# New weights for the budget that spreads the PEER routing over the expert tiles, and six gathered slots moved behind the routing

## The chip, the cores and the metric

One core of a Trainium2 chip runs one decoder layer as one program. The metric is the device time in microseconds (us) of an execution, the median of three runs of the kernel before. The engines are named as the profile names them: PE is TensorE (PEld its weight loads), DVE is VectorE, ACT is ScalarE, POOL is GpSimd, SP is SyncE, whose queue starts most of the transfers between HBM and SBUF.

## The reference

A layer on 512 tokens of width 1024, in float32: attention beside a Conformer convolution, then the part that this case is about, PEER, then a gated embedding and a last RMSNorm. PEER retrieves from 128 x 128 experts of one neuron each:

```python
q = (xb @ w_q).reshape(P, PEER_HEADS, 2, PEER_DK_HALF)
s = jnp.einsum('phcd,hcnd->phcn', q, sub_keys)
v1, i1 = lax.top_k(s[:, :, 0], 16);  v2, i2 = lax.top_k(s[:, :, 1], 16)
cand = v1[..., :, None] + v2[..., None, :]          # 16 x 16 sums a head
best, pos = lax.top_k(cand.reshape(P, 8, 256), 16)
e, g = cand_idx[pos], softmax(best)                 # 8 x 16 = 128 slots a token
act = gelu(einsum('pd,phkd->phk', xb, u_tab[e]))
out = einsum('phk,phkd->pd', g * act, v_tab[e])
```

## The kernel before, in words

The 512 tokens are four token tiles of 128. Everything up to the scores of the keys is done by some 334 us of the span. From there the kernel does PEER in two ways.

**Token tiles 1 to 3 go dense.** The 16384 experts are 128 expert tiles of 128. For every expert tile, `dense_act` (lines 788 to 799) multiplies its slice of `u_t` by the 384 tokens (24 matmuls into `aps`, three for each product, since each float32 operand is split into a high and a low part) and ACT puts the GELU of it into a tile `act`. Later `dense_out` (line 1054) multiplies the gated `act` by the expert tile's slice of `v_tab` (18 matmuls into `vps`). In front of each, `stage` (line 775) loads the slice (`tr`), ACT rounds it to the high part (`th`) and DVE makes the low part (`tl`, line 144). `act` is a ring of 19 buffers (RING). I write A0, A1, ... for `dense_act` of the k-th expert tile and V0, V1, ... for `dense_out` in its order.

**The gates of the dense way are the routing.** `route` (line 984) is a generator of small pieces for one token tile after the other: `best_keys` (16 pieces: the 16 best of 128 keys, L723 to L728), `topk` (8 pieces for the 8 heads, L859 to L864; then one-hot compares that turn positions into expert numbers, L900 to L911, into a tile `sel` with one buffer). For token tiles 1 to 3 follow three PE transposes (L929 to L931), which ACT copies to `ids` and `gsc` (L933, L936), and 16 halves of a scatter: DVE makes one-hot tiles `o12` (L950) and gated ones `og` (L957), two buffers each, PE multiplies them (`gp`, L977 and L978, 16 matmuls a half), ACT copies the result to `stg` (L979), and SP writes `gd` to HBM (L982).

**Token tile 0 is gathered.** Its 128 slots are fetched row by row by POOL (L808 from `u_tab`, then L819 from `v_tab`), with four buffers `g`; DVE does one pass a row (`gj`, L812, then `acc`, L822): 256 slots in all.

**What sets the order.** The first stage is the loop of lines 998 to 1013: 65 expert tiles A0 to A64, and behind each as much of the routing as a budget allows. `vec` adds up the DVE time of what was written, `mat` the PE time, both from constants and from the weights that the pieces yield; pieces are taken while `vec < pace * mat`, where `pace` is the ratio of the sums expected for the whole stage (line 995). G_EARLY gathered slots are spread over it from the tile G_FROM on. `tiles_later(2)` holds the transposes and the first scatter of a token tile back until two more expert tiles are written; while it does, keys of the next token tile are taken. The transposes and each half's matmuls are tied behind the last matmul of the expert tile written last (`tc.issue_after`, lines 928 and 974). Everything else is an order of priority only: the framework's planner lets an instruction that is ready go ahead of an earlier one that is not, on each engine, at times that it works out itself. `prep_act(e + 2)` stands two tiles ahead of its use.

Written behind the loop, `units` (line 1076 on) are A65, A66, A67, V0, A68, V1, ...: `prep_out` (line 1042) of V0 needs the gates of all three token tiles, loaded from `gd` (`gch`, L1034, three pieces at first), times `act` (`cf`, L1047), split into `ch` (ACT) and `cl` (DVE). The ring has room for A65 and A66 beside the 17 kept tiles; A67 gets its buffer when V0's `cf` has read its own. `background` (line 1068, called after each unit) spreads the remaining gathered slots evenly by weight, G_EARLY of them taken as done.

Of the kernel before, what the change touches and what calls it, by code (L numbers as in the profile page):

```python
# [55 lines left out]
OCH = 8  # L56
PAIR = 2
GBUF = 4
G_EARLY = 6
G_FROM = 20  # L60
EARLY_TOP = (0, 1)
TOP_PACE = 4
ROUTE_V = 237.0
ROUTE_M = 46.0
U_V = 1.2
G_V = 1.25
A_M = 3.9
CONV_PE = (1,)
TAPS = (6, 2, 5, 2)
FILL = (2, 2, 1.5, 1.5, 1, 1, 1, 1)  # L70
# [27 lines left out]
def hymba_layer(ctx, tc, x, xT, p_t, pos, pvec, conv_ln_g, conv_ln_b, w_in, w_uq, w_ukv, w_out,  # L98
# [48 lines left out]
    def split(hi, lo, src, g=None):  # L147
        split_hi(hi, src, g)
        split_lo(lo, src, hi, g)
# [9 lines left out]
    def rows(w, k, c0, c1):  # L159
        return w[k * P:(k + 2) * P, c0:c1].rearrange("(i p) n -> p i n", p=P)  # L160

    def wpair(srcs, n, gains, beside=None):

        r = wst.tile([P, 2, 512], F32, name="wr2", tag="wr")
        hi = wst.tile([P, 2, 512], F32R, name="wh2", tag="wh", bufs=WBUF)
        lo = wst.tile([P, 2, 512], F32R, name="wl2", tag="wl", bufs=WBUF)
        for i in (slice(0, 1), slice(1, 2)) if beside else (slice(0, 2),):
            if beside:
                nc.sync.dma_start(*beside[i.start])
            o = 0  # L170
            for src in srcs:
                w = src.shape[-1]
                nc.sync.dma_start(r[:, i, o:o + w], src[:, i])
                o += w
        if gains is None:
            split(hi[:, :, :n], lo[:, :, :n], r[:, :, :n])
        else:
            for i in range(2):
                split(hi[:, i, :n], lo[:, i, :n], r[:, i, :n], gains[i])
        return hi, lo  # L180
# [6 lines left out]
    with ExitStack() as fs:  # L187
# [414 lines left out]
        for s in range(n_it + 7):  # L602
            if s < n_it:
                t, h = items[s]
# [104 lines left out]
    def new_top(t):  # L709
        tops[t] = (hpool.tile([P, NH, 2, TOPK], F32, name=f"tv{t}", tag="tv", bufs=2),  # L710
                   hpool.tile([P, NH, 2, TOPK], U32, name=f"ti{t}", tag="ti", bufs=2))

    with ExitStack() as fs:
        ps_mm = fs.enter_context(tc.tile_pool(name="ps_mm", bufs=4, space=PSUM))
        mid = fs.enter_context(tc.tile_pool(name="mid", bufs=1))

        def best_keys(t, rs):
            if t not in tops:
                new_top(t)
            s, (tv, ti) = sc[t], tops[t]  # L720
            for r in rs:
                h, c = divmod(r, 2)
                nc.vector.max(out=tv[:, h, c, 0:8], in_=s[:, r])  # L723
                nc.vector.max_index(out=ti[:, h, c, 0:8], in_max=tv[:, h, c, 0:8], in_values=s[:, r])
                nc.vector.match_replace(out=s[:, r], in_to_replace=tv[:, h, c, 0:8], in_values=s[:, r],
                                        imm_value=-3e38)
                nc.vector.max(out=tv[:, h, c, 8:16], in_=s[:, r])
                nc.vector.max_index(out=ti[:, h, c, 8:16], in_max=tv[:, h, c, 8:16], in_values=s[:, r])  # L728
                yield 1.0, 0.0

        early = (i for t in EARLY_TOP for i in best_keys(t, range(8)))


        for g in range(2):
            kraw = mid.tile([P, 4, 2 * NK], F32, name="kraw", tag="kraw")
            nc.vector.memset(kraw, 0.0)
            nc.sync.dma_start(kraw[0:64, :, 0:NK], keys_t[0][:, g * 4:g * 4 + 4])
            nc.sync.dma_start(kraw[64:128, :, NK:], keys_t[1][:, g * 4:g * 4 + 4])
            kbh = mid.tile([P, 4, 2 * NK], F32R, name="kbh", tag="kbh")
            kbl = mid.tile([P, 4, 2 * NK], F32R, name="kbl", tag="kbl")  # L740
            split(kbh, kbl, kraw)
            qTh = mid.tile([P, 4, T], F32R, name="pqh", tag="pqh")
            qTl = mid.tile([P, 4, T], F32R, name="pql", tag="pql")
            ps = [ps_mm.tile([P, 512], F32, name="qps", tag="mm") for _ in range(4)]
            for k2 in range(0, KD, 2):
                if g:
                    for _ in range(TOP_PACE):
                        next(early, None)
                hi, lo = wpair([rows(peer_wq, k2, g * 512, g * 512 + 512)], 512, None)
                for i in range(2):  # L750
                    k = k2 + i
                    for j in range(4):
                        mm3(ps[j], hi[:, i, j * P:(j + 1) * P], lo[:, i, j * P:(j + 1) * P], xnh[:, k], xnl[:, k],
                            k == 0, k == KD - 1)
            for j in range(4):
                split(qTh[:, j], qTl[:, j], ps[j])
            for t in range(NT):
                for j in range(0, 4, 2):
                    h = g * 4 + j
                    ps = ps_mm.tile([P, 512], F32, name="sps", tag="mm")  # L760
                    for i in range(2):
                        mm3(ps[:, i * 256:(i + 1) * 256], qTh[:, j + i, t * P:(t + 1) * P],
                            qTl[:, j + i, t * P:(t + 1) * P], kbh[:, j + i], kbl[:, j + i], True, True)
                    nc.scalar.activation(sc[t][:, 2 * h:2 * h + 4].rearrange("p a n -> p (a n)"), ps, AF.Copy)
        for _ in early:
            pass
# [58 lines left out]
    with ExitStack() as fs:  # L825
# [14 lines left out]
        def tiles_later(n):  # L840

            e = last_tile[0] + n
            while last_tile[0] < e:
                yield None

        def topk(t):
# [11 lines left out]
            for h in range(NH):  # L858
                nc.vector.max(out=bv[:, h, 0:8], in_=cand[:, h])  # L859
                nc.vector.max_index(out=bp[:, h, 0:8], in_max=bv[:, h, 0:8], in_values=cand[:, h])  # L860
                nc.vector.match_replace(out=cand[:, h], in_to_replace=bv[:, h, 0:8], in_values=cand[:, h],
                                        imm_value=-3e38)
                nc.vector.max(out=bv[:, h, 8:16], in_=cand[:, h])
                nc.vector.max_index(out=bp[:, h, 8:16], in_max=bv[:, h, 8:16], in_values=cand[:, h])  # L864
                yield (1.9 if h == 0 else 0.8), 0.0

            ge = tmp.tile([P, NH, TOPK], F32, name="ge", tag="ge")
            nc.vector.tensor_tensor(ge, bv, bv[:, :, 0:1].to_broadcast([P, NH, TOPK]), op=ALU.subtract)
# [26 lines left out]
            for j0, w in ((0, 8), (8, 16)):  # L895
# [14 lines left out]
                for c in range(2):  # L910
# [7 lines left out]
            pg = pg0 if t == 0 else tmp.tile([P, NSL], F32, name="pg", tag="pg")  # L918
            nc.vector.tensor_tensor(pg.rearrange("p (h k) -> p h k", h=NH), ge,
                                    gs.unsqueeze(2).to_broadcast([P, NH, TOPK]), op=ALU.mult)  # L920
            yield 1.0, 0.0
            if t == 0:
                nc.vector.scalar_tensor_tensor(pidx, sel[:, 0], float(NK), sel[:, 1], op0=ALU.mult, op1=ALU.add)
                return
# [17 lines left out]
            for c in range(P // TCH):  # L942
                stg = s8p.tile([P, NK, TCH], F32, name="stg", tag="s8")
                for c0 in range(0, TCH, OCH):
                    cs = slice(c * TCH + c0, c * TCH + c0 + OCH)
                    ng = OCH // PAIR
                    gs0 = cs.start // PAIR
                    o12 = ohp.tile([P, ng, 2, NK, PAIR], F16, name="o12", tag="o12")
                    og = ohp.tile([P, ng, 2, NK, PAIR], F16, name="og", tag="og")
                    nc.vector.tensor_tensor(  # L950
                        o12.rearrange("p g c n q -> p (g c) n q"),
                        iok.unsqueeze(1).to_broadcast([P, 2 * ng, NK, PAIR]),
                        ids[:, gs0:gs0 + ng].rearrange("p g c q -> p (g c) q").unsqueeze(2)
                        .to_broadcast([P, 2 * ng, NK, PAIR]), op=ALU.is_equal)
                    yield 1.1, 0.0

                    nc.vector.tensor_tensor(  # L957
                        og, o12[:, :, 1].unsqueeze(2).to_broadcast([P, ng, 2, NK, PAIR]),
                        ghl[:, gs0:gs0 + ng].unsqueeze(3).to_broadcast([P, ng, 2, NK, PAIR]), op=ALU.mult)
                    late.append((c, c0, stg, o12, og))  # L960
                    if len(late) > LATE:
                        if not started:

                            yield from tiles_later(2)
                            started = True
                        scatter(t, *late.pop(0))
                    yield 1.1, 0.94
            while late:
                scatter(t, *late.pop(0))

# [23 lines left out]
        ngat, vec, mat = 0, 0.0, 0.0  # L994
        pace = (ROUTE_V + U_V * EARLY + G_V * G_EARLY) / (A_M * (EARLY - 2) + ROUTE_M)
        for e in range(AHEAD):
            prep_act(e)
        for e in range(EARLY):
            prep_act(e + AHEAD)
            dense_act(e)  # L1000
            vec += U_V
            mat += A_M
            want = (e + 1 - G_FROM) * G_EARLY / (EARLY - G_FROM)
            while ngat < want:
# [14 lines left out]
    with ExitStack() as fs:  # L1019
# [48 lines left out]
        def background(w):  # L1068
            nonlocal ngat, spent
            spent += w  # L1070
            want = G_EARLY + spent / total * (2 * NSL - G_EARLY)
            while ngat < 2 * NSL and ngat < want:
# [226 lines left out]
```

## Time and profile before

| | |
|---|---|
| median of three runs | 1523.48 us (1522.2 to 1530.78) |
| the profiled execution | 1526.01 us, span 1524.1 us, mean granted clock 0.989 |
| PE busy | 1481.5 us (97%), 8070 matmuls |
| PEld busy | 1317.8 us (86%) |
| DVE busy | 1263.0 us (83%) |
| ACT busy | 715.1 us (47%) |
| POOL busy | 416.0 us (27%) |
| chain that ended last | PE 73%, DVE 18%, ACT 5%, issue 2%, DMA 1% |

A busy engine is one with an instruction running; matmuls overlap, so a PE that is busy all the time is not at its peak, but a PE that is idle has lost that time. The profiled execution is 1.9 us longer than its span, and 2.5 us over the median of the runs.

### The profile page before, as it was taken

To read this page: it belongs to the slowest core of one execution; us is meant where nothing else is said; L and a number is where in the kernel's file an instruction comes from. 1 tells how busy PE (TensorE), PEld (TensorE's weight loads), DVE (VectorE), ACT (ScalarE), POOL (GpSimd) and SP (SyncE) were. 2 spreads that over 40 slices of the span, in tenths; PEclk is the share of its full clock that TensorE was granted. 3 is DMA by queue.
4 is the path that set the end of the run, shared out by engine and by line. 5 is a ranking of instruction groups with operands and counts; after the bars stand their busy time and mean duration, and the time that the engine had idled before them with its cause. 6 is when DMAs were issued, how large, how long until landed. Compare 5 with 4: busy or idle time off the path is not lost.

```text
span 1524.1 us, 22835 instructions
## 1 busy us (share of the span) xinstructions
PE 1481.5 (97%) x8070; PEld 1317.8 (86%) x8070; DVE 1263.0 (83%) x2566; ACT 715.1 (47%) x1160; POOL 416.0 (27%) x302
## 2 busy tenths in 40 slices
PE   7999989999979999999999999999999999999997
PEld 6888868789979899999999999999999888888886
DVE  5999674699999997977868887886888798888776
ACT  7467873444457484753333332333333333333454
POOL 0010010001000000014545554554555373444000
PEclk9999989999999999999999999999999999999998
DMA  7331114525558575589999999999999999998562
GB/s 224 99 98 56 43 42 173 200 70 185 178 196 303 188 288 192 224 323 359 334 361 318 345 332 348 342 339 351 316 340 327 383 379 390 351 372 287 197 193 97
DMA packets 143474, 386.55 MB, mean 254 GB/s; under 512 B 13696, under 2 KB 58112, under 8 KB 140288
## 3 DMA queue, kind: packets, MB, share of 16 engines
q1 hardware_dynamic: 105920, 249.82, 47.1%
q0 software_dynamic: 36864, 134.23, 24.3%
q8 instruction: 63, 1.03, 0.3%
q10 hardware_dynamic: 576, 1.05, 0.2%
q14 instruction: 51, 0.42, 0.1%
HBM read 343.63 MB, written 41.42 MB: 253 GB/s over the span
## 4 chain that ended last, share of the span: by engine, by line
PE 73%; DVE 18%; ACT 5%; issue 2%; DMA 1%; POOL 0%; SPq 0%; ACTq 0%; POOLq 0%; DVEq 0%
PE vps L153 12%; PE vps L154 12%; PE vps L152 11%; PE aps L154 8%; PE aps L152 8%; PE aps L153 8%; DVE tl L144 3%; DVE cacc L308 2%; PE bank L153 2%; PE bank L154 2%; PE bank L152 2%; DVE o L950 1%; DVE og L957 1%; PE qps L152 1%; PE qps L153 1%
## 5 line engine op out<-in xcount | busy, mean ns | idle before, releaser
L139 ACT ACTIVATE th<-tr 128x1024 fp32r<-128x1024 f32 x256 | 270.7, 1058 | 439.7 <-DMA tr<-in_u_t 190.3
L144 DVE SCALAR_TENSOR_TENSOR tl<-tr,th 128x1024 fp32r<-128x1024 f32 x256 | 311.6, 1218 | 90.0 <-ACT th L139 89.7
L152 PE MATMUL aps<-mixh,th 128*128 128x384 f32 x1024 | 345.4, 337 | 1.9 <-ACT act L795 1.9
L154 PE MATMUL aps<-mixh,tl 128*128 128x384 f32 x1024 | 344.4, 336 | 0.0
L153 PE MATMUL aps<-mixl,th 128*128 128x384 f32 x1024 | 343.8, 336 | 0.0
L808 POOL DMA_INDIRECT gu<-in_u_tab,pidx x128 | 183.6, 1435 | 541.3 <-DVE gj L812 332.8
L154 PE MATMUL vps<-th,cl 128*128 128x512 f32 x768 | 300.1, 391 | 0.0
L153 PE MATMUL vps<-tl,ch 128*128 128x512 f32 x768 | 300.1, 391 | 0.0
L152 PE MATMUL vps<-th,ch 128*128 128x512 f32 x768 | 298.9, 389 | 0.0
L819 POOL DMA_INDIRECT gv<-in_v_tab,pidx x128 | 205.1, 1602 | 202.4 <-DVE acc L822 187.3
L152 PEld LDWEIGHTS aps<-mixh,th 128*128 128x128 f32 x1024 | 192.6, 188 | 4.6 <-ACT act L795 2.2
L153 PEld LDWEIGHTS aps<-mixl,th 128*128 128x128 f32 x1024 | 192.5, 188 | 2.3
L154 PEld LDWEIGHTS aps<-mixh,tl 128*128 128x128 f32 x1024 | 192.4, 188 | 0.0
L822 DVE SCALAR_TENSOR_TENSOR acc<-gv,gact,acc 128x1024 f32<-128x1024 f32 x128 | 163.7, 1279 | 17.4 <-DMA gv<-in_v_tab,pidx 16.7
L812 DVE SCALAR_TENSOR_TENSOR gj<-gu,xn 128x1024 bf16<-128x1024 f32 x128 | 156.3, 1221 | 24.9 <-DMA gu<-in_u_tab,pidx 23.7
L154 PEld LDWEIGHTS vps<-th,cl 128*128 128x128 f32 x768 | 144.1, 188 | 29.9
L153 PEld LDWEIGHTS vps<-tl,ch 128*128 128x128 f32 x768 | 144.1, 188 | 29.2 <-DVE tl L144 0.3
L152 PEld LDWEIGHTS vps<-th,ch 128*128 128x128 f32 x768 | 144.2, 188 | 28.6
L139 ACT ACTIVATE ch<-cf 128x384 fp32r<-128x384 f32 x128 | 66.7, 522 | 173.9 <-PE vps L153 96.4
L979 ACT ACTIVATE stg<-gp 128x512 f32<-128x512 f32 x96 | 94.2, 1117 | 26.5 <-PE gp L978 22.4
L144 DVE SCALAR_TENSOR_TENSOR cl<-cf,ch 128x384 fp32r<-128x384 f32 x128 | 70.7, 553 | 27.2 <-ACT ch L139 27.2
L141 ACT ACTIVATE wh<-wr,pv 128x512 fp32r<-128x512 f32 (+2 forms) x84 | 54.8, 693 | 47.3 <-PE bank L154 27.4
(300 smaller groups left out, 2183.7 us busy)
## 6 DMA issues: line engine op xcount, KB each, us to landing
tr<-in_u_t SPq DMA_DIRECT2D x128, 512.0 KB, 5.6
tr<-in_v_tab SPq DMA_DIRECT2D x128, 512.0 KB, 6.5
gd<-stg SPq DMA_DIRECT2D x24, 1024.0 KB, 4.5
gch<-gd SPq DMA_DIRECT2D x84, 256.0 KB, 10.9
ad<-act SPq DMA_DIRECT2D x48, 192.0 KB, 3.9
aback<-ad SPq DMA_DIRECT2D x48, 192.0 KB, 6.6
wr<-in_gate_w SPq DMA_DIRECT2D x12, 512.0 KB, 3.8
wr<-in_w_out SPq DMA_DIRECT2D x8, 512.0 KB, 3.2
```

The lines of the kernel that those rows point to most:

```text
L139: nc.scalar.activation(hi, src, AF.Copy)
L141: nc.scalar.activation(hi, src, AF.Copy, scale=g)
L144: nc.vector.scalar_tensor_tensor(lo, src, 1.0 if g is None else g, hi.bitcast(F32), op0=ALU.mult, op1=ALU.subtract)
L152: nc.tensor.matmul(ps, lh, rh, start=first, stop=False)
L153: nc.tensor.matmul(ps, lh, rl, start=False, stop=False)
L154: return nc.tensor.matmul(ps, ll, rh, start=False, stop=last)
L308: nc.vector.scalar_tensor_tensor(cacc[:, c], yT[:, c, j:j + T], tap(c, j), cacc[:, c], op0=ALU.mult, op1=ALU.add)
L808: nc.gpsimd.indirect_dma_start(out=g, out_offset=None, in_=u_tab, in_offset=bass.IndirectOffsetOnAxis(ap=pidx[:, s:s + 1], axis=0))
L812: nc.vector.scalar_tensor_tensor(junk, g, 1.0, xn0, op0=ALU.mult, op1=ALU.mult, accum_out=gact[:, s:s + 1]))
L819: nc.gpsimd.indirect_dma_start(out=g, out_offset=None, in_=v_tab, in_offset=bass.IndirectOffsetOnAxis(ap=pidx[:, s:s + 1], axis=0))
L822: nc.vector.scalar_tensor_tensor(acc0, g, gact[:, s:s + 1], acc0, op0=ALU.mult, op1=ALU.add))
L979: nc.scalar.activation(stg[:, :, c0 + q:c0 + q + 4].rearrange("p n t -> p t n"), gp, AF.Copy, scale=1.0 / GSC)
```

## The change

Constants and weights alone change; no instruction is added or taken away. The budget's sums for the routing, the split on DVE and the expert tile on PE, and the weights of five kinds of pieces, are set to other values. G_EARLY becomes 0: no gathered slot is written in the first stage, and all 256 are spread over the second.

```diff
-G_EARLY = 6
+G_EARLY = 0
...
-ROUTE_V = 237.0
-ROUTE_M = 46.0
-U_V = 1.2
+ROUTE_V = 229.0
+ROUTE_M = 47.0
+U_V = 1.13
 G_V = 1.25
-A_M = 3.9
+A_M = 4.16
...
                 nc.vector.max_index(out=ti[:, h, c, 8:16], in_max=tv[:, h, c, 8:16], in_values=s[:, r])
-                yield 1.0, 0.0
+                yield 1.13, 0.0
...
-                yield (1.9 if h == 0 else 0.8), 0.0
+                yield (1.7 if h == 0 else 0.9), 0.0
...
-            yield 1.0, 0.0
+            yield 0.6, 0.0
             if t == 0:
...
-                    yield 1.1, 0.0
+                    yield 1.12, 0.0
...
-                    yield 1.1, 0.94
+                    yield 1.12, 0.98
```

## Rows read from the trace of the kernel before

**Rows 1.** Waits of PE: us in total, times, longest; 334 to 690 us.
```profile
PE gp L977 <- DVE og L957: 12.1, 7, 5.9
PE aps L152 <- ACT act L795: 1.9, 1, 1.9
```

**Rows 2.** Busy us (instructions) of the engines, PE clock, DMA share, GB/s, by stretch.
```profile
571.00:610.00 39.00, 39.00 (x231) 38.97 (x229) 27.78 (x100) 18.06 (x24) 0.94 (x1) 1.00 0.57 197
...
689.00:1196.00 507.00, 507.00 (x2559) 460.97 (x2559) 414.55 (x542) 175.07 (x242) 263.69 (x181) 1.00 0.95 341
```

**Rows 3.** Timeline of PE where it waited: start, us, instruction, [idle before <-releaser].
```profile
429.22 0.23 PE L977 MATMUL gp<-og,o 128*128 128x128 f16 x1 [1.55 <-DVE og L957]
...
441.35 0.29 PE L977 MATMUL gp<-og,o 128*128 128x128 f16 x1 [5.87 <-DVE og L957]
...
522.62 0.23 PE L977 MATMUL gp<-og,o 128*128 128x128 f16 x1 [1.18 <-DVE og L957]
...
531.25 0.24 PE L977 MATMUL gp<-og,o 128*128 128x128 f16 x1 [2.53 <-DVE og L957]
```

**Rows 4.** Timelines: low part of A4, A20 on DVE; its first use on PE.
```profile
344.43 1.23 DVE L144 SCALAR_TENSOR_TENSOR tl<-tr,th 128x1024 fp32r<-128x1024 f32 x1
...
354.57 0.33 PE L154 MATMUL aps<-mixh,tl 128*128 128x384 f32 x1
...
419.38 1.21 DVE L144 SCALAR_TENSOR_TENSOR tl<-tr,th 128x1024 fp32r<-128x1024 f32 x1
...
423.70 0.33 PE L154 MATMUL aps<-mixh,tl 128*128 128x384 f32 x1
```

**Rows 5.** Timelines: expert numbers of token tiles 1, 2 leave ACT, DVE takes them.
```profile
416.17 0.38 ACT L933 ACTIVATE ids<-str 128x256 f16<-128x256 f32 x1
...
425.33 0.23 DVE L937 CAST ghl<-gsc 128x128 f16<-128x128 f32 x1
...
513.97 0.37 ACT L933 ACTIVATE ids<-str 128x256 f16<-128x256 f32 x1
...
518.74 0.22 DVE L937 CAST ghl<-gsc 128x128 f16<-128x128 f32 x1
```

**Rows 6.** Line L723 alone, one for each key piece: DVE busy (count), clock, DMA.
```profile
482.40:517.60 35.20, 3.61 (x13) 1.00 0.63 212
```

**Rows 7.** Timeline of DVE between the second and third half of token tile 2.
```profile
523.62 1.22 DVE L144 SCALAR_TENSOR_TENSOR tl<-tr,th 128x1024 fp32r<-128x1024 f32 x1
...
526.58 1.20 DVE L144 SCALAR_TENSOR_TENSOR tl<-tr,th 128x1024 fp32r<-128x1024 f32 x1
```

**Rows 8.** Timeline of PE: first, last scatter of token tile 3; V0's first `cl`.
```profile
618.19 0.24 PE L977 MATMUL gp<-og,o 128*128 128x128 f16 x1
...
659.07 0.22 PE L978 MATMUL gp<-og,o 128*128 128x128 f16 x1
...
689.46 0.40 PE L154 MATMUL vps<-th,cl 128*128 128x512 f32 x1
```

**Rows 9.** Timelines of SP's queue and DVE from the last scatter to V0.
```profile
661.69 0.32 SPq L982 DMA_DIRECT2D gd<-stg  x1
...
665.85 2.57 SPq L1034 DMA_DIRECT2D gch<-gd  x3
...
677.61 1.03 DVE L1047 TENSOR_TENSOR cf<-act,gch 128x384 f32<-128x384 f32 x2 [0.50 <-DMA gch<-gd]
678.88 0.56 DVE L144 SCALAR_TENSOR_TENSOR cl<-cf,ch 128x384 fp32r<-128x384 f32 x1 [0.25 <-ACT ch L139]
...
680.50 1.22 DVE L144 SCALAR_TENSOR_TENSOR tl<-tr,th 128x1024 fp32r<-128x1024 f32 x1
```

**Rows 10.** Busy us by stretch, as in Rows 2, behind the longest wait.
```profile
441.30:447.00 5.70, 5.66 (x36) 5.66 (x37) 5.70 (x21) 1.98 (x2) 0.00 (x0) 0.75 0.41 130
```

**Rows 11.** Timelines of DVE and PE: the low part of V65 and its use.
```profile
1206.80 1.22 DVE L144 SCALAR_TENSOR_TENSOR tl<-tr,th 128x1024 fp32r<-128x1024 f32 x1
...
1208.07 0.50 PE L153 MATMUL vps<-tl,ch 128*128 128x512 f32 x1
```

## The prediction

> **What bounds the kernel now.** Read the share of busy time first: PE 97%, so the kernel can only become shorter where PE is idle or where its order changes. The list of PE's waits between 334 and 690 us, the stage that the change reorders, then says how much there is: 12.1 us in 7 waits of scatter matmuls for `og` from DVE, and 1.9 us in one wait for ACT [rows 1]. From 689 to 1196 us PE is busy every microsecond [rows 2], and no wait on `vps` stands in the list. So the prize is at most 14.0 us, 0.9% of the time.
>
> The timeline of PE puts the waits where token tile 1 begins its scatter (1.55 and 5.87 us, with small ones 7.9 in all) and where token tile 2 does (1.18 and 2.53, 4.2 in all); token tile 3 has none [rows 3]. The waits are a lag of DVE that has built up before. The low part of A4 is ready 8.9 us before its first use, that of A20 only 3.1 us [rows 4]: with the 1.9 us that PE lost in between, DVE falls back (8.9 - 3.1 + 1.9) / 16 = 0.48 us with each expert tile of (423.70 - 354.57 - 1.9) / 16 = 4.2 us. When ACT has made the expert numbers of token tile 1, DVE comes to them 9 us later, for token tile 2 it is 4.5 us later [rows 5]. That lag is what PE waits for at the first halves; afterwards both stand level, and it builds up again.
>
> **What the change moves.** Nothing is added or removed, so all of it is order. Running the budget's own sums by hand gives the places. `pace` goes from (237 + 1.2 x 65 + 1.25 x 6) / (3.9 x 63 + 46) = 1.106 to (229 + 1.13 x 65) / (4.16 x 63 + 47) = 0.979. Before, transposes and first scatter are written behind A17 and A20 for token tile 1, A34 and A36 for tile 2, A52 and A54 for tile 3; the trace has them there. After, they are behind A19 and A22, A38 and A40, A56 and A58: 2, 4 and 4 expert tiles later.
>
> Does DVE get less work per tile with the lower pace? I hold that it does not, or little. The weights only set priorities; the planner puts any ready piece into a free place. The 13 keys that DVE does between 482.4 and 517.6 us [rows 6] are keys 1 to 13 of token tile 3, and 8 of them are written behind A41 to A43, five to seven tiles later than PE stood then. So DVE is filled to what the planner takes for its capacity, before as after, and it falls back by the same 0.48 us a tile as long as ready routing is left.
>
> Term by term:
>
> 1. Token tile 1. Two more filled tiles ahead of its scatter add 2 x 0.48 = 1.0 us to a lag that cost 7.9. What stood between its second and third half (a gathered slot of 1.2 us among it) is replaced by other ready pieces, selections of tile 2. I take +1.0; the ends are -7.9 (no lag left) and +2.
> 2. Token tile 2. From the end of tile 1's scatter to its own transposes DVE had 8 expert tiles; it gets 10. In 35.2 us it did 7 splits of 1.2 and 27 us of other work [rows 4, 6], 3.4 us a tile, so there is place for 34 us. The work: 27, less the 7 already done in the two extra tiles, plus two keys (2.3) and the selection of tile 3 as far as the one `sel` buffer lets it. That selection is most of the 27.8 us between 571 and 610, less 9 splits and a slot, about 15 [rows 2], perhaps 12 of it allowed. That makes 34: used up just in time. The first wait (1.2, with the small ones 1.7) stays, for the lag of 10 tiles less a little idle. The second one goes: the third half stood behind two keys and two splits, 523.62 to 527.70 [rows 7], and no key is left to stand there. I take -2.5; ends -4.2 and +1.9 (four tiles at 0.48).
> 3. Token tile 3. DVE is idle ahead of it in either order (27.8 of 39 us [rows 2]), so no wait: 0. The wait for ACT before A13 lies where nothing moves: 0. The same table switch for tile 3's softmax, which ACT now meets with a lag, has the end +1.9.
> 4. The six slots. In the first stage they took DVE places that are filled again (inside term 1 and 2). In the second stage 256 instead of 250 slots are spread, 2.4% more, beside a DVE that is 82% busy while PE never waits [rows 2]. Its thinnest place is V65, whose low part is ready 0.05 us before its use [rows 11]. +0.3; ends 0 and +1.
> 5. The handover to the second stage. This is where a cover goes. Token tile 3's last scatter ends at 659.07, with A61 to A67 behind it before V0 (30 us) [rows 8]. The chain from it: ACT's copies, the write of `gd` at 661.69, the three `gch` loads at 665.85, `cf` at 677.61, `cl` ready at 679.44 [rows 9]. V0 uses `cl` at 689.46, a margin of 10.0 us. The scatter begins four expert tiles later and takes as long, since DVE sets its pace, so the chain comes 4 x 4.2 = 16.8 us later against V0: 6.8 us late. A68, whose slice needs no gates, could go in front of V0 and give 4.2 back: 2.6. If the V0 slice itself is loaded behind the waiting `gch` on SP's queue, as it was before, its low part (ready at 681.72, used one matmul before 689.46) has 7.5 us of margin and is 9.3 late. A67 is no way out for more: its `act` buffer waits for the same `cf`. I take +4.5, between 2.6 and 6.8; ends 0 and 9.3.
> 6. The clock. After the 5.87 us wait the granted clock is 0.75 over 5.7 us [rows 10], part of it at 1.2 GHz, which costs 0.25 x 5.7 = 1.4 us. After 2.53 us there is no such loss. An idle of 4.5 lies between: +0.5; ends 0 and 1.4.
>
> The price of the `gch` loads can be read otherwise. The rows have 11.8 us from the issue of three loads of 1 MB to the first `cf` [rows 9]. The Trainium skill (DMA: Bandwidth & Descriptors, Anatomy of one DMA — SWDGE (gpsimd) path) gives for another path of issue 2.0 us and the bytes by 436 GB/s, an estimate of 2.0 + 7.2 = 9.2 us; by it term 5 would be some 2.6 smaller and the sum +1.2. The sum goes by the trace, whose loads run beside other transfers.
>
> Sum: 1.0 - 2.5 + 0 + 0.3 + 4.5 + 0.5 = +3.8. From the profiled 1526.0 that is 1529.8; it is 2.5 over the median of the runs, so on the runs 1523.5 + 3.8 = 1527.3, and I say 1527.
>
> **The rivals.**
>
> *The budget does pace DVE.* Then 0.979 instead of 1.106 leaves no lag, all 14.0 us of waits go, and of the handover between 0 and 4.5 stays: 1509.5 to 1514, say 1513. For it: every wait in the list is DVE being late, and pace falls by 11%, the size of the lag (0.48 in 4.2). Against it: the keys done far ahead of their place.
>
> *The handover bites in full (slower).* SP's queue holds V0's slice behind `gch`, PE stands 9.3 us, the clock falls for 1.4, and tiles 1 and 2 keep their waits (+1.0, and 0): 1523.5 + 12.0 = 1535.5. It decides as soon as less than 30.4 - 10.0 = 20.4 us of expert tiles stand behind the last scatter; I count 13.6. Against it: with the scatter so late, V0's load may well be issued ahead of `gch`, and A68 may fill in.
>
> *Nothing shows.* The waits stay as they are, and A68 with quicker loads covers the handover: 1523.5 + 0.8 = 1524.
>
> **How the numbers follow.** My forecast has 0.45 (1522 to 1532 as its own range), the budget 0.22, the handover in full 0.20, nothing 0.13. What a measurement can tell from no change is 0.5%, 7.6 us: under 1515.9 is faster, over 1531.1 slower. Faster has nearly all of the budget's case, 0.21. Slower has most of the handover's, 0.18, and 0.06 of the forecast's upper end: 0.24. The rest, 0.55, is the same. The range of 8 in 10 reaches from the budget's value to the handover's, 1512 to 1536.
>
> **What would show it.** In the profile after: first scatters behind A22, A40 and A58 (if not, the whole count falls); PE's waits for `og` at tile 1 of 8 to 9 us, at tile 2 under 2 us with no wait at its third half; low parts still losing some 0.5 us a tile up to A22; at the handover a PE idle of 2 to 7 us before V0 or a V0 behind A68, with `cf` as its releaser. The forecast is wrong if the waits for `og` are gone, if PE shows no idle between A65 and V0, or if a wait on `vps` appears in the second stage.

## The result and the profile after

The changed kernel takes 1539.68 us (median of 6 runs, 1536.78 to 1543.26), against 1528.93 us for the kernel before on the same chip: a ratio of 1.0088, 95% interval 1.0072 to 1.0104. (The two medians alone give 1.0070; the mean over the pairs of executions behind the first is 1.0088.) It is slower, by more than the 0.5% bound; 1527 was forecast, with a range to 1536. Of the 12.7 us above the forecast, 5.4 are not the change's: the kernel before took 1528.9 us here, and the forecast starts from 1523.5. One of the twelve executions of e10 below took 8413.97 us, counts as slow and stands in no ratio. The profiled execution took 1538.39 us (span 1536.5), 12.4 us more than the one before. The places came as counted: first scatters behind A22, A40 and A58.

DVE falls back as before. In the changed kernel the low parts of A4 and A22 on DVE and their first uses on PE, against [rows 4]:

```profile
343.25 1.22 DVE L144 SCALAR_TENSOR_TENSOR tl<-tr,th 128x1024 fp32r<-128x1024 f32 x1
...
353.39 0.33 PE L154 MATMUL aps<-mixh,tl 128*128 128x384 f32 x1
...
427.62 1.22 DVE L144 SCALAR_TENSOR_TENSOR tl<-tr,th 128x1024 fp32r<-128x1024 f32 x1
...
430.83 0.33 PE L154 MATMUL aps<-mixh,tl 128*128 128x384 f32 x1
```

The margin goes from 8.9 to 2.0 us, and PE lost 1.9 in between: (8.9 - 2.0 + 1.9) / 18 = 0.49 us a tile, where the prediction had 0.48.

PE's waits in the first stage of the changed kernel, in total (answers to [rows 1]):

```profile
PE gp L977 <- DVE og L957: 12.6, 4, 7.9
PE vps L152 <- ACT ch L139: 4.8, 1, 4.8
PE aps L152 <- ACT act L795: 3.5, 2, 1.9
```

The same waits on PE's timeline, against [rows 3]. The row at 541.80 is token tile 2's first half, that at 549.82 its third; the last three rows are V0's first matmuls:

```profile
437.59 0.23 PE L977 MATMUL gp<-og,o 128*128 128x128 f16 x1 [2.79 <-DVE og L957]
...
450.56 0.29 PE L977 MATMUL gp<-og,o 128*128 128x128 f16 x1 [7.93 <-DVE og L957]
...
533.27 0.45 PE L152 MATMUL aps<-mixh,th 128*128 128x384 f32 x1 [1.61 <-ACT act L795]
...
541.80 0.23 PE L977 MATMUL gp<-og,o 128*128 128x128 f16 x1
...
549.82 0.24 PE L977 MATMUL gp<-og,o 128*128 128x128 f16 x1 [1.55 <-DVE og L957]
...
699.47 0.79 PE L152 MATMUL vps<-th,ch 128*128 128x512 f32 x1 [4.79 <-ACT ch L139]
700.06 0.63 PE L153 MATMUL vps<-tl,ch 128*128 128x512 f32 x1
700.49 0.63 PE L152 MATMUL vps<-th,ch 128*128 128x512 f32 x1
```

Waits for `og` are hardly more than before (12.6 against 12.1) but lie otherwise: token tile 1 has 10.7 instead of 8.1, tile 2 has 1.9 instead of 4.0. (The prediction splits the 12.1 into 7.9 and 4.2; this small wait of the kernel before is tile 1's.)

```profile
461.30 0.23 PE L977 MATMUL gp<-og,o 128*128 128x128 f16 x1 [0.22 <-DVE og L957]
```

Two waits are new: 1.6 for ACT while it makes tile 3's softmax, 4.8 before V0. The granted clock behind the two longest (columns as in [rows 2]; answers to [rows 10]):

```profile
446.00:456.40 10.40, 5.84 (x39) 5.53 (x39) 9.38 (x12) 7.90 (x10) 0.00 (x0) 0.51 0.45 172
698.70:705.50 6.80, 6.03 (x14) 4.78 (x15) 6.55 (x13) 2.64 (x5) 2.88 (x3) 0.50 0.93 307
```

Both stretches ran at 1.2 GHz. The first costs (1 - 0.51) x 5.84 = 2.9 us; in the second each of V0's first 14 matmuls (of 18) takes 0.43 us from start to start instead of 0.23, 2.8 us. Before, the only such loss was 1.3.

The handover, on the timelines of PE (last scatter), SP's queue and DVE, against [rows 8, 9]:

```profile
676.20 0.22 PE L978 MATMUL gp<-og,o 128*128 128x128 f16 x1
...
676.35 0.33 SPq L778 DMA_DIRECT2D tr<-in_v_tab  x1
...
678.77 0.32 SPq L982 DMA_DIRECT2D gd<-stg  x1
...
683.77 8.42 SPq L1034 DMA_DIRECT2D gch<-gd  x4
...
698.17 1.03 DVE L1047 TENSOR_TENSOR cf<-act,gch 128x384 f32<-128x384 f32 x2 [5.48 <-DMA gch<-gd]
```

V0's slice is issued ahead of the gate loads, and A68 runs in front of V0. The write of `gd` comes 17.1 us later than before, as counted (16.8). The loads then take 14.4 us to `cf`, not 11.8. The stretch of these loads, the kernel before first:

```profile
665.85:677.61 11.76, 11.76 (x70) 11.76 (x69) 5.36 (x7) 3.37 (x5) 1.49 (x1) 1.00 1.02 330
```
```profile
683.77:698.17 14.40, 10.91 (x63) 10.59 (x62) 3.06 (x3) 2.50 (x3) 0.00 (x0) 1.00 1.08 371
```

DMA is full in both (share 1.02 and 1.08). In the changed kernel 371 GB/s x 14.4 us = 5.3 MB move in this stretch, in the kernel before 330 x 11.76 = 3.9 MB: the loads share the DMA engines with more. I take that for the reason; no run changed the traffic alone.

Last, waits in the second stage, where the kernel before has none:

```profile
811.80 0.44 PE L152 MATMUL aps<-mixh,th 128*128 128x384 f32 x1 [1.37 <-ACT act L795]
...
812.68 0.45 PE L154 MATMUL aps<-mixh,tl 128*128 128x384 f32 x1 [0.26 <-DVE tl L144]
...
817.84 0.50 PE L153 MATMUL vps<-tl,ch 128*128 128x512 f32 x1 [0.84 <-DVE tl L144]
```

| us | predicted | traces |
|---|---|---|
| 1 waits at tile 1 | +1.0 | +2.6 |
| 2 waits at tile 2 | -2.5 | -2.1 |
| 3 ACT at tile 3's softmax | 0 | +1.6 |
| 4 waits in the second stage (slots) | +0.3 | +2.5 |
| 5 PE idle before V0 | +4.5 | +4.8 |
| 6 half clock (2.9 + 2.8 - 1.3) | +0.5 | +4.4 |
| sum | +3.8 | +13.8 |

The first expert tile began 1.2 us earlier in the execution after, which makes 12.6, beside the 12.4 that the executions differ by.

### The profile page after: what moved, and what is told of

Same layout as the page of the kernel before. It is cut to its first block, busy times and chain, and to the rows that moved or that the text cites. A ratio compares the mean times of both kernels' runs of the same rounds, so it can differ in the third digit from the quotient of the medians.

```text
span 1536.5 us, 22834 instructions
## 1 busy us (share of the span) xinstructions
PE 1484.0 (97%) x8070; PEld 1320.3 (86%) x8070; DVE 1263.0 (82%) x2566; ACT 716.0 (47%) x1160; POOL 416.5 (27%) x302
## 4 chain that ended last, share of the span: by engine, by line
PE 56%; issue 24%; DVE 8%; DMA 6%; ACT 4%; POOL 1%; SPq 0%; POOLq 0%; ACTq 0%; DVEq 0%
PE vps L153 10%; PE vps L154 10%; PE vps L152 10%; PE aps L154 4%; PE aps L152 4%; PE aps L153 4%; DMA gu<-in_u_tab,pidx 4%; DVE cacc L308 2%; PE bank L152 2%; PE bank L153 2%; PE bank L154 2%; PE qps L152 1%; POOL gu L808 1%; PE qps L153 1%; PE qps L154 1%
## 5 line engine op out<-in xcount | busy, mean ns | idle before, releaser
L819 POOL DMA_INDIRECT gv<-in_v_tab,pidx x128 | 208.5, 1629 | 192.1 <-DVE acc L822 169.0
```

The lines of the kernel that those rows point to most:

```text
L819: nc.gpsimd.indirect_dma_start(out=g, out_offset=None, in_=v_tab, in_offset=bass.IndirectOffsetOnAxis(ap=pidx[:, s:s + 1], axis=0))
```

## The experiments

Ratios are to the kernel before, with 95% intervals, from 5 to 12 executions of each version; what is read from a trace is read from one of them.

**Which part carries it.** First the two halves of the change alone, then the changed kernel with token tile 3 written early again.

Weights alone (e1):
```diff
-G_EARLY = 0
+G_EARLY = 6
```


> The changed kernel with G_EARLY back at 6: the new weights alone. The scatters of token tiles 1, 2, 3 begin behind A21, A41 and A58 and the last one of tile 3 still ends in A64. Theory (order of the routing: lag at tile 1, too little behind the last scatter, half clock behind both waits): as slow as the changed kernel within 3 us, so some 1.006 to 1.010 of the kernel before; PE idle at tile 1 of 9 to 11 us and before V0 of 4 to 6 us. Rival (the six slots moved into the second stage cost the time): back to 1.000 to 1.003, and no waits of PE near 810 us.


Measured: 1.0079 (1.0058 to 1.0100); 5.4 us idle before V0, 13.9 us of waits for `og`. Putting the slots back gains nothing that shows against 1.0088.

Slots alone, in the kernel before (e2):
```diff
-G_EARLY = 6
+G_EARLY = 0
```


> The kernel before with G_EARLY = 0: the six slots moved, old weights. Scatters begin behind A21, A38 and A54, the last one of tile 3 ends in A60 as before. Theory: handover free (no PE idle before V0), tile 1 with 0.5 to 1 us more lag, tile 2 with no key left between its halves, so within 0.998 to 1.003 of before. Rival (the slots are the cost): 1.005 or more, with the waits near 810 us.


Measured: 1.0056 (1.0034 to 1.0077). A miss: `G_EARLY` stands in `pace` too (1.106 becomes 1.080), so the scatters moved and waits for `og` rose to 16.1 us. The ratio is the rival's, but of its waits near 810 us there is none (2.7 us lie at 942 us and later). It didn't isolate the slots; e8 does.

Tile 3 early (e3):
```diff
-            while vec < pace * mat:
+            while vec < (pace if e < 50 else 2.0) * mat:
```


> The changed kernel, but from the 51st expert tile on all that is left of the routing is written at once: tile 3's transposes and scatter stand behind A52 and A54 as before, tiles 1 and 2 as in the changed kernel. Theory: the idle before V0 (4.8 us) and the half clock behind it (2.8 us) go, 7 to 8 us less than the changed kernel: 1.003 to 1.005 of before. Rival (the gates were not the cause of the wait at the handover): same as the changed kernel, 1.008 to 1.010.


Measured: 1.0026 (1.0013 to 1.0038). No idle before V0: 0.62% of the 0.88% goes with the place of tile 3.

The mirror, tile 3 alone late in the kernel before (e7):
```diff
-            yield from tiles_later(2)
+            yield from tiles_later(6 if t == 3 else 2)
```


> The kernel before, with only token tile 3's transposes and scatter held back to the places that they have in the changed kernel (behind A56 and A58). Theory (the handover is a loss by itself: 4 to 7 us idle before V0 and 2 to 3 us of half clock after it): +7 to +10 us, ratio 1.004 to 1.007, with tiles 1 and 2 as in the kernel before. Rival (the loss at the handover needs the rest of the change, A68 or V0's load covers it): within 0.2% of before.


Measured: 1.0054 (1.0033 to 1.0075). Tiles 1 and 2 wait as before; V0 starts after 4.99 us of idle and at half clock. The handover is a loss of some 8 us by itself.

The slots alone, with weights and order as before (e8):
```diff
-G_EARLY = 6
+G_EARLY = 0
+G_PLAN = 6
...
-        pace = (ROUTE_V + U_V * EARLY + G_V * G_EARLY) / (A_M * (EARLY - 2) + ROUTE_M)
+        pace = (ROUTE_V + U_V * EARLY + G_V * G_PLAN) / (A_M * (EARLY - 2) + ROUTE_M)
...
-            want = (e + 1 - G_FROM) * G_EARLY / (EARLY - G_FROM)
+            want = (e + 1 - G_FROM) * G_PLAN / (EARLY - G_FROM)
             while ngat < want:
-                next(gu, None)
...
+        ngat = 0
```


> The kernel before with its own weights, and so with the scatters at their old places, but with the six gathered slots issued in the second stage instead of the first. It tells what the slots cost where they land from what their leaving does to the order ahead of the scatters. Theory (what the slots-only kernel lost was the lower pace and shifted scatters): 0 to +3 us, ratio 0.999 to 1.002, waits of 0 to 3 us on vps or aps in the second stage. Rival (256 instead of 250 slots in the second stage overload DVE): +6 us and more, ratio 1.004 or above, with most of it as PE waits behind V0.


Measured: 1.0020 (1.0007 to 1.0034), 3.4 us of waits in the second stage. The longest of them, 1.6 us at 1209, is followed by half clock: 0.72 over the 6 us from there, some 1.5 us. Beside the kernel before the slots cost some 3 us.

What is left, the new weights with tile 3 early and the slots in the first stage (e13):
```diff
-G_EARLY = 0
+G_EARLY = 6
...
-            while vec < pace * mat:
+            while vec < (pace if e < 50 else 2.0) * mat:
```


> The changed kernel's weights, with token tile 3 where it was (behind A52 and A54) and the six slots in the first stage: what is left of the change is the later place of tiles 1 and 2 and the order of the pieces. Theory (the loss is the handover and the slots, and little else): within 0.15% of the kernel before, ratio 0.999 to 1.0015. Rival (the lower pace costs by itself, through tile 1's longer wait and the half clock after it): ratio 1.002 to 1.004, with waits for og of 10 us and more at tile 1.


Measured: 1.0031 (1.0019 to 1.0044). The ratio is the rival's: the new places of tiles 1 and 2 with the new order cost 4.7 us. Its wait at tile 1 is 9.6 us, not 10, and 2.3 us more stand in the second stage. Beside e3 (1.0026) the slots are worth nothing here. So the sum closes, roughly, as handover 0.5 to 0.6%, tiles 1 and 2 with what follows them 0.3%; what the slots cost depends on the rest.

Tile 1 alone (e9), then tile 2 alone (e10), held back in the kernel before:
```diff
-            yield from tiles_later(2)
+            yield from tiles_later(4 if t == 1 else 2)
```


> The kernel before, with only token tile 1's transposes and scatter held back by the two expert tiles that the change moves them. Theory (two more tiles of falling behind, and a longer half clock behind the longer wait): PE waits for og at tile 1 of 9 to 11.5 us instead of 8.1, half clock after it longer by 3 to 7 us, +2 to +5 us in all, ratio 1.001 to 1.004, tile 2 as in the kernel before. Rival (tile 1's greater loss came from the new order of the pieces, not from the later place): waits of 8 to 8.5 us, ratio 0.999 to 1.001.


Measured: 0.9986 (0.9973 to 0.9999), waits for `og` 12.3 against 12.1. My theory fell, the rival's 8.5 us at tile 1 came: the later place costs nothing, it is even 0.14% faster, the only version here whose interval lies (just) under the kernel before. So, by elimination, tile 1's loss belongs to the new order of pieces that comes with the weights; no run changed the order alone.

```diff
-            yield from tiles_later(2)
+            yield from tiles_later(6 if t == 2 else 2)
```


> The kernel before, with only token tile 2's transposes and scatter held back by the four expert tiles that the change moves them. Theory (this part of the change is a gain: the second wait goes, the first stays): waits for og at tile 2 from 4.2 to 1 to 2 us, ratio 0.997 to 0.9995. Rival (four tiles more of falling behind show somewhere else, at tile 2's scatter, in ACT's softmax of tile 3, or in the second stage): ratio 1.000 to 1.003, with a wait of 1.5 us or more that the kernel before has not.


Measured: 1.0007 (0.9990 to 1.0023). PE's timeline at tile 2:

```profile
536.40 0.44 PE L152 MATMUL aps<-mixh,th 128*128 128x384 f32 x1 [2.43 <-ACT act L795]
...
543.98 0.23 PE L977 MATMUL gp<-og,o 128*128 128x128 f16 x1 [3.15 <-DVE og L957]
```

The waits for `og` shrink from 4.0 to 3.2, and 2.43 us for ACT appear: the later place gives back what it takes, as the rival had it.

**The clock.** Does the idle before V0 cost twice? Dummy matmuls in the two longest waits of the changed kernel (e5; a second `warm` for V0 writes into `vps`):
```diff
+WARM = 60
+WARM_V = 50
+        def warm(n):
+            w = ps_tr.tile([P, 512], F32, name="warm", tag="tr")
+            with tc.issue_after(last_tile[1]):
+                for _ in range(n):
+                    nc.tensor.matmul(w[:, :TD], xnh[:, 0, :P], xnh[:, 0, P:], start=True, stop=True)
...
+            if (t, c, c0) == (1, 1, 0):
+                warm(WARM)
...
+            if first:
+                warm(WARM_V)
```


> The changed kernel with dummy matmuls (128x384, fp16, results never read; nothing of the output changes) that fill PE's two longest waits: 60 ahead of token tile 1's third half, 50 ahead of V0. Theory (part of the loss is half clock after PE's idle, 2.9 us after the 7.9 us wait and 2.8 us after the 4.8 us wait): the waits themselves remain as time, filled or not, but the granted clock no longer falls behind them, so 3 to 6 us less than the changed kernel, about 1535 of its 1539.7, ratio to before 1.004 to 1.007. Rival (the clock is not what the idle costs, or the dummy work lengthens the waits it fills): the same as the changed kernel or up to 8 us slower, ratio 1.008 to 1.014.


Measured: 1.0128 (1.0106 to 1.0151), inside the rival's bounds. At tile 1 the dummies did not fill the wait but displaced it (PE's timeline, the dummies as `warm`):

```profile
437.45 10.68 PE L977 MATMUL warm<-mixh 128*128 128x384 f32 x60
...
460.35 0.29 PE L987 MATMUL gp<-og,o 128*128 128x128 f16 x1 [5.62 <-DVE og L959]
```

The wait of 5.6 us is still there and ends 12 us behind the dummies, with selections and keys on DVE in between; I take it that the planner counts PE as busy and lets DVE do other routing first. So this place says nothing on the clock. The place ahead of V0 does (PE's timeline, then the 8.7 us from V0's start on, columns as in [rows 2]):

```profile
693.66 8.83 PE L1067 MATMUL vps<-mixh 128*128 128x384 f32 x50
```
```profile
703.29:712.00 8.71, 8.71 (x43) 7.76 (x44) 7.00 (x13) 2.84 (x6) 4.05 (x4) 1.00 1.07 368
```

With that idle filled but for 0.8 us, V0 ran at a clock of 1.00, where the changed kernel had 0.50; what the dummies displaced at tile 1 hides the gain in the time. The clean form for the time, e7 with 28 dummies between A68 and V0 (e11):
```diff
+WARM_V = 28
...
-            yield from tiles_later(2)
+            yield from tiles_later(6 if t == 3 else 2)
...
+            if first:
+                warm(WARM_V)
...
+        units[FREE + 1:FREE + 3] = units[FREE + 1:FREE + 3][::-1]
```


> Token tile 3 alone late, as in the run of that name, and 28 dummy matmuls (128x384, fp16, 4.9 us, results never read; nothing of the output changes) between A68 and V0, where PE stood idle for 5.0 us. Theory (what follows the idle is the clock): V0 starts where it started, 0 to 1 us later, and its matmuls run at 2.4 GHz from the first, which saves the 2.7 us of half clock: ratio 1.003 to 1.004 where the run without the dummies had 1.0054, and a second stage of 779 to 780 us where that one had 782.7. Rival (V0's first matmuls are slow for another reason, such as its operands' arrival): the same 2.7 us lost behind V0's start, ratio 1.005 to 1.006.


Measured: 1.0035 (1.0022 to 1.0049), beside 1.0054 without. V0's first 6.8 us without dummies, then its first 6.5 us with them (columns as in [rows 2]), and PE's timeline with them:

```profile
695.20:702.00 6.80, 5.84 (x14) 4.64 (x15) 6.55 (x12) 2.64 (x5) 2.69 (x2) 0.52 0.92 305
```
```profile
699.50:706.00 6.50, 6.10 (x26) 4.89 (x27) 6.25 (x12) 2.48 (x6) 2.95 (x3) 1.00 0.85 283
```
```profile
699.90 0.50 PE L153 MATMUL vps<-th,ch 128*128 128x512 f32 x1 [1.65 <-ACT ch L140]
...
700.83 0.40 PE L153 MATMUL vps<-th,ch 128*128 128x512 f32 x1
701.06 0.39 PE L154 MATMUL vps<-tl,ch 128*128 128x512 f32 x1
```

26 matmuls instead of 14 in that time, soon at 0.23 us a step: the operands were there, it was the clock. The two intervals overlap, so the trace shows this and the times only agree. Part of the gain went elsewhere: V0 began 6.5 us behind A68's last matmul instead of 5.0, more than the 0 to 1 us expected, and the second stage has waits of 2.0 us where e7 has 0.3.

**Can DVE be kept from working ahead?** Routing pieces held to the place where the budget writes them, in the changed kernel (e4); then with tile 3 early and ACT's softmax held as well (e6):
```diff
+    pin = tc.keep_in_program_order
...
-                nc.vector.max(out=tv[:, h, c, 0:8], in_=s[:, r])
+                pin(nc.vector.max(out=tv[:, h, c, 0:8], in_=s[:, r]))
...
-            nc.vector.tensor_tensor(cand[:, :, 0:16], v1[:, :, 0:1].to_broadcast([P, NH, 16]), v2, op=ALU.add)
+            pin(nc.vector.tensor_tensor(cand[:, :, 0:16], v1[:, :, 0:1].to_broadcast([P, NH, 16]), v2, op=ALU.add))
...
-                nc.vector.max(out=bv[:, h, 0:8], in_=cand[:, h])
+                pin(nc.vector.max(out=bv[:, h, 0:8], in_=cand[:, h]))
```


> The changed kernel with every piece of key and head selection pinned behind the DVE instruction written before it, so that it can't be put into a free place ahead of its turn; placement of the scatters unchanged (A22, A40, A58). Theory (the lag comes from pieces put ahead of their turn): the low parts keep 7 us or more of margin at A20, the waits for og at tile 1 fall from 10.7 to under 3 us with no half clock there, the handover still costs 7 to 8: some 10 to 13 us less than the changed kernel, 1.000 to 1.002 of before. Rival (DVE is simply too slow for the budget's pace, or its dependent instructions stall when nothing is put between them): waits at tile 1 of 8 us or more again, and the time as the changed kernel or more.


Measured: 1.0071 (1.0053 to 1.0089). Waits for `og` fall from 12.6 to 3.5 us, as they should if they were DVE being ahead elsewhere. It isn't shown by that alone: PE now stands 5.6 us for ACT (its exp waits for DVE's late `ge`) at 407.8, ahead of tile 1's scatter, which gives DVE that time; and 5.1 before V0.

```diff
-            nc.scalar.activation(ge, ge, AF.Exp)
+            pin(nc.scalar.activation(ge, ge, AF.Exp))
...
-            while vec < pace * mat:
+            while vec < (pace if e < 50 else 2.0) * mat:
```


> The changed kernel with tile 3 written by the old budget (its scatter behind A55 again, so the handover is free) and with routing pieces of DVE and the softmax's exp of ACT held to the place where the budget writes them. Theory (PE waits at tiles 1 and 2 because DVE and ACT take routing ahead of its place): waits for og and for ACT fall from 14.2 us to under 5 us, no idle before V0, no long half clock: 8 to 14 us below the kernel before is not to be had, 4 to 9 us is, ratio 0.994 to 0.998. Rival (DVE simply has too much to do ahead of tile 1, wherever it is held): waits of 8 us and more stay in the first stage, ratio 1.000 to 1.005.


Measured: 1.0084 (1.0058 to 1.0111). Both missed: waits for `og` 7.6, but 6.7 of transposes for `sel` and `pg`, and 6.0 in the second stage. As I read it, what DVE doesn't do ahead it owes later.

A version meant to beat both, dense work between the second and third half (e12):
```diff
+HOLD3 = 1
...
-            yield from tiles_later(2)
+            yield from tiles_later(6 if t == 2 else 2)
...
+                        if t < 3 and c * TCH + c0 == 3 * OCH:
+                            yield from tiles_later(HOLD3)
                         scatter(t, *late.pop(0))
```


> A version meant to beat both: the kernel before, with tile 2's scatter four expert tiles later, and at tiles 1 and 2 one expert tile written between the second and the third half of the scatter, so that PE has 4.2 us of dense work while DVE makes the third half. Theory (PE waits there because DVE has other routing ahead of that half, and the wait can be covered by dense work): the 5.9 us wait of tile 1 falls to under 2.5 us, the half clock after it goes, waits for og of 3 to 5 us in all instead of 12.1: -6 to -9 us, ratio 0.994 to 0.997. Rival (the planner fills the room with more routing of the next tile, so the half comes later by as much): waits of 9 us or more remain, ratio 0.998 to 1.002.


Measured: 0.9999 (0.9984 to 1.0014), the rival's value, though waits at tile 1 only move:

```profile
428.10 0.23 PE L980 MATMUL gp<-og,o 128*128 128x128 f16 x1 [1.55 <-DVE og L958]
440.25 0.23 PE L980 MATMUL gp<-og,o 128*128 128x128 f16 x1 [1.68 <-DVE og L958]
445.85 0.29 PE L980 MATMUL gp<-og,o 128*128 128x128 f16 x1 [4.50 <-DVE og L958]
```

**What repeats.** Both kernels unchanged, one execution each (e14, e15).


> The kernel before, unchanged, profiled a second time: it shows what belongs to a single execution. Theory (the order of the first stage repeats to 0.1 us, the clock's answer doesn't): the same waits for og (1.55, 5.87, 1.18, 2.53 us within 0.1), half clock after the 5.87 us wait of 3 or 7 us, and after the 2.53 us one of 0 or 3.5 us; waits of 0 to 2 us in the second stage. Rival (all of it repeats): half clock 3.4 us after the first and none after the second, and no wait in the second stage.


Measured: 1525.69 us. Waits of the first stage within 0.1 us, none in the second, and the clock's loss repeats too (1.4 and 1.3): the rival holds.


> The changed kernel, unchanged, profiled a second time. Theory: the waits of tile 1 (2.8 and 7.9 us), of ACT (1.6) and before V0 (4.8) come again within 0.3 us, since the order sets them; the half clock behind them lasts 3, 7 or 10 us, and the waits near V14 to V16 are between 0 and 3 us. Rival: the half clock of 10.2 us at tile 1 and 6.8 us behind V0's start and 2.5 us of waits in the second stage come again as they were.


Measured: 1544.45 us. PE's waits from V0 on:

```profile
PE vps L152 <- ACT ch L139: 5.8, 1, 5.8
PE vps L153 <- DVE tl L144: 3.5, 5, 0.8
PE vps L152 <- ACT th L139: 0.4, 1, 0.4
PE aps L152 <- ACT act L795: 0.4, 1, 0.4
PE aps L154 <- DVE tl L144: 0.3, 1, 0.3
```

Tile 1 and ACT repeat within 0.1 us, the idle before V0 is 5.8 instead of 4.8, the second stage has 4.5 us of waits instead of 2.5. The half clock again costs 2.9 and 2.5. The loss isn't that of one execution.

## Why the prediction was wrong

**The step that failed is term 6, the clock: +0.5, with 1.4 as its upper end, measured +4.4** (and +4.0 in the second pair of executions, 2.9 + 2.5 - 1.4). I put a price on one new idle, the one before V0, between that of a wait of 2.5 us (nothing) and of 5.9 (1.4), and nothing on a longer one at tile 1. The idle of 4.8 before V0 cost 2.8, twice the price of the longer one, and the wait at tile 1, grown to 7.9, cost 2.9 instead of 1.3. The lower clock was known; that it could last twice as long was not in the bounds. e5 and e11, which fill the idle before V0, show it as the cause there; at tile 1 it is read from the trace, since no experiment took it away there, and there it can't be put down to the longer wait: waits of 5.9 cost 2.9 too in two executions (see the last section). Term 6 is the largest part of the miss, 3.9 us of the 10.0 between the two sums; waits at tile 1, for ACT and in the second stage (1.6, 1.6 and 2.2 more than taken) are most of the rest.

**The handover, term 5**, was right in its mechanism: 4.5 taken, 4.8 measured, and e3 and e7 show that it is a loss by itself, with the clock behind it 0.5 to 0.6% of the 0.88%. That the number is so near is partly luck, for its parts were off in both directions. The chain was 4.2 + 4.8 = 9.0 us late instead of 6.8, mainly since the gate loads took 2.6 us more; A68 in front took its full 4.2 off, of which the 4.5 had counted about half. The estimate that I had worked out there from the Trainium skill (DMA: Bandwidth & Descriptors, Anatomy of one DMA — SWDGE (gpsimd) path), 9.2 us for the three loads, is further off than the trace before: 14.4 was measured. The rival of the handover in full came nearest (1535.5) by another way than its own: V0's slice was not held behind `gch`.

**Token tile 1, term 1** (+1.0, measured +2.6, end +2) and **the ACT wait, term 3** (0, measured +1.6, end +1.9): right in sign, and in that the lower budget doesn't relieve DVE (0.49 us a tile), but e9 shows that the working was wrong. Two more tiles alone add 0.4 us of waits, not 1.0; the rest comes, by elimination, with the other order of pieces under the new weights. I treated places as if the order stayed.

**Token tile 2, term 2**: -2.5, measured -2.1, and that is luck. The first wait was to stay and that of the third half to go; it came the other way round, with no wait at 541.80 and 1.55 us at 549.82. Nor is it the place alone: e10 gains 0.9 there and loses 2.4 for ACT.

**The slots, term 4**: +0.3, with end +1; the second stage got 2.5 us of waits. They are not the slots' doing alone, for e1, e9, e11 and e13 keep the slots in the first stage and wait 1.3 to 2.3 us there. Why the stage, which had no wait in two executions of the kernel before, has them behind most changes ahead of it (not in e5, e10 and e12) is not settled. Many lie near 810 us, beside the reading of its second chunk of gates, others near 950 and 1210; no run tested either. A wait on `vps` in this stage (817.84) was one of my own signs that the forecast is wrong.

**The rival that the budget paces DVE** (1513) is refuted: waits for `og` stay at 12.6. The terms that I had at or near nothing (ACT, slots, clock) all came out on the slow side, and the range ended at the handover's rival, which has them at 0, +0.3 and 1.4.

## What to carry to other kernels

For each wait of TensorE that you add or lengthen, put into the range its length plus a stretch at half clock; here 4.8 us of idle cost 7.6. Before you write work later by a budget, count what stands behind its last piece against the chain that hangs on it (gates written, read back, multiplied, split), with transfers priced as beside full DMA (14.4 us here for three loads that took 11.8 before). And weights of a planner don't only move places: they can reorder what fits between, so test the place and the order apart.

## What was not expected

The clock's answer to one and the same wait differs. Five executions with an identical first stage up to there wait 5.87 to 5.89 us at tile 1; the 8 us after it (columns as in [rows 2]), first the kernel before twice, then e7, e10 and e11:

```profile
441.35:449.35 8.00, 7.54 (x56) 7.09 (x56) 8.00 (x26) 2.78 (x3) 0.00 (x0) 0.83 0.57 206
```
```profile
440.75:448.75 8.00, 7.63 (x56) 7.18 (x56) 8.00 (x26) 2.79 (x3) 0.00 (x0) 0.82 0.66 211
```
```profile
439.17:447.17 8.00, 7.74 (x56) 7.29 (x56) 8.00 (x26) 2.79 (x3) 0.00 (x0) 0.80 0.62 192
```
```profile
440.82:448.82 8.00, 8.00 (x49) 7.84 (x50) 7.97 (x25) 2.00 (x3) 0.00 (x0) 0.64 0.62 204
```
```profile
439.53:447.53 8.00, 8.00 (x47) 7.84 (x48) 7.96 (x25) 1.98 (x2) 0.00 (x0) 0.62 0.64 217
```

A clock of 0.80 to 0.83 in three executions, 0.62 to 0.64 in two: 56 matmuls done against 47 to 49. An idle of this length has two prices here, some 1.4 and some 2.9 us. e11 also lost 1.7 us behind tile 2's wait of 2.53, which cost nothing in the kernel before.

Shorter idles can cost it too. The wait for ACT before A13, 1.9 us long in both, cost no clock in the changed kernel but did in e3, which is written the same up to there (the 3.3 us behind the wait, the changed kernel first):

```profile
392.54:395.84 3.30, 3.24 (x19) 3.25 (x20) 3.30 (x12) 1.34 (x3) 0.00 (x0) 1.00 0.46 166
```
```profile
390.90:394.20 3.30, 3.24 (x10) 3.25 (x11) 3.30 (x12) 1.33 (x3) 0.00 (x0) 0.51 0.54 166
```

e5 shows a like loss at that place. What decides between the two is open; the length of the idle alone doesn't.
